# Second product of the second block's MLP by 2x2 blocks: seven block products per group in place of eight

## The chip, the cores and the metric

The kernel runs on one core of a Trainium2 chip. The core has TensorE (PE) for matrix products, which reads SBUF and writes PSUM; VectorE (DVE), ScalarE (ACT) and GpSimd (POOL) for elementwise work; and SyncE (SP), which here issues the loads of the weights. Each engine takes its instructions in order, and waits at the head of its own queue for semaphores of the others. The metric is the device time of one execution in microseconds (us); less is better. A measurement of this kernel can tell about 0.5% (some 6 us) from no change.

## The reference, cut to what matters

Two transformer blocks run one after the other on 512 tokens of width 1024, in float32. The change lies in the MLP of the second block, whose hidden width is 4096:

```
def _sq_relu_mlp(h, w1, w2):
    return jnp.square(jax.nn.relu(h @ w1)) @ w2
```

Its result is normalised by its rms, multiplied by a gain and added to the tokens; that is the kernel's output.

## The kernel before

**Products.** Every float32 operand is held as two parts, hi + lo, that TensorE takes in one pass each (`split`, L146: ACT copies the high part, L147, and DVE subtracts it for the low part, L148). A product is then three matmuls, hi·hi, hi·lo and lo·hi (`mm3`, L150 to L154).

**The MLP** (`mlp`, called by `dense_two`, name m2). The hidden width is 32 chunks of 128. `up(j)` makes chunk j of the first product, 128 hidden columns for all 512 tokens: 24 matmuls of 512 columns (for the first five chunks 48 of 256). ACT takes the relu (L843), DVE multiplies (L844), and the result is split into hi and lo in a tile `hid` of four chunks; three such tiles rotate. After eight chunks the second product of the group follows: two halves of 512 output columns, four tiles of 128 tokens, eight chunks, three matmuls each, so 192 matmuls for a group and 768 in all. The sum of a group stays in PSUM; ACT copies the first group's to `y` (L1278) and DVE adds the later ones to it (L1280). `y` is one tile [128, 1024] for each 128 tokens.

**Weights.** Each weight tile [128, 1024] comes by a DMA of 512 KB from SP's queue into one of two buffers (`raw`), and is split by ACT and DVE into hi and lo tiles, five of each (`wh`, `wl`). In the first four chunks of each MLP GpSimd does the subtraction in DVE's place (`WPJ`). In this MLP a tile of the first product serves 24 matmuls and one of the second product 24.

**The order.** A scheduler orders each engine's queue when the kernel is built; the program is written chunk by chunk and group by group. GpSimd has nothing from the fourth chunk of this MLP until the sums of squares at its end.

**The end.** With the last group, done token tile by token tile, `evac2` takes the sum of squares of `y` (ACT, L1243), multiplies by the gain (DVE, L1288), gets 1 / rms (GpSimd, L1245 to L1248), adds to the tokens (DVE, L1255) and stores.

Of the kernel before, what the change touches and what calls it, by code (L numbers as in the profile page):

```python
# [129 lines left out]
class Build:  # L130
    def __init__(self, tc, a, out):
        self.tc, self.nc, self.a, self.out = tc, tc.nc, a, out
        self.last_turn = None

# [1 line left out]
    def ps(self, tag, name):  # L136
        """the next of the tag's banks"""
# [7 lines left out]
    def split(self, hi, lo, src, eng=None):  # L145
        """src = hi + lo exactly, both parts fit the one-pass format"""  # L146
# [3 lines left out]
    def mm3(self, out, lh, ll, rh, rl, start, stop):  # L150
        mm = self.nc.tensor.matmul
# [10 lines left out]
    def weights(self, name, srcs, a, b, gain=None, eng=None):  # L162
        """hi/lo parts [128, a, b] of weights (times a gain [128, a] of the rows); srcs: (column offset, DRAM view [128, a, width])"""
# [82 lines left out]
    def columns(self, name, rows):  # L246
        """rows of the modulation, 128 columns to a partition"""
# [980 lines left out]
    def dense_two(self):  # L1228
# [46 lines left out]
        def evac2(grp, half, t, acc):  # L1275
            cols = slice(half * 512, half * 512 + 512)
            if grp == 0:
                ac(out=y[t][:, cols], in_=acc, func=AF.Copy)  # L1278
                return
# [40 lines left out]
```

## Time and profile before

| | us |
|---|---|
| median of three runs | 1274.99 |
| the three runs | 1271.56, 1274.99, 1276.72 |
| span of the profiled execution | 1270.8 |
| start of the second product's first matmul, group 0 | 951.81 |
| end of the last matmul | 1263.1 |
| busy in the whole span: PE / DVE / ACT / POOL | 1227.1 / 750.8 / 539.2 / 257.5 |

No time is given for the profiled execution itself other than its span; the span lies 4.2 us under the median of the runs, since it leaves out what lies before the first and behind the last instruction, and since executions differ. The MLP in question takes the span from about 910 us to its end. Busy times are read engine by engine in a stretch of time; "x" is the number of instructions. A matmul is recorded with its latency (0.39 us), and the next one begins 0.23 us later, so their cost is read from the distance of their starts.

### The profile page before, as it was taken

The page shows a single profiled execution, that of the slowest core. Times are in us where ns is not written, and L with a number is a line of the kernel's source. Part 1 is how long each engine was busy: PE and PEld are TensorE (multiplying, and loading weights), DVE is VectorE, ACT ScalarE, POOL GpSimd, SP SyncE. Part 2 cuts the span into 40 slices and gives each one's busy share as a digit, 9 for nine tenths or more (in the row PEclk, how much of TensorE's full clock was granted, in tenths as well). Part 3 has the DMA queues.
Part 4 walks back from the last instruction along what each step waited for, and adds up shares of the span by engine and source line. Part 5 has one row for each costly group of instructions (what it writes and reads, how often), then busy time and mean ns, then how long its engine had stood idle before and what let it go on. Part 6 is the DMA issues. An engine that isn't in the chain of part 4 may idle for free. (4 is left out here: it accounts for less than half of the span.)

```text
span 1270.8 us, 16908 instructions
## 1 busy us (share of the span) xinstructions
PE 1227.1 (97%) x6388; PEld 1027.8 (81%) x6388; DVE 750.8 (59%) x1320; ACT 539.2 (42%) x1032; POOL 257.5 (20%) x328
## 2 busy tenths in 40 slices
PE   7889999999999999999999999999999999999997
PEld 7889887779888788888888777778888888888886
DVE  4799666597897854336364567564752343433534
ACT  6677555434223324235263556454652331422431
POOL 3877551261020000000023114212400000000001
PEclk9899999999999999999999999999999999999999
DMA  5232121464678733143254122215232322412412
GB/s 163 64 73 68 26 63 67 133 186 148 198 239 257 234 100 116 63 131 122 67 176 129 51 67 74 64 59 178 82 117 83 100 100 67 130 69 67 149 50 84
DMA packets 147290, 140.22 MB, mean 110 GB/s; under 512 B 14025, under 2 KB 115160, under 8 KB 147208
## 3 DMA queue, kind: packets, MB, share of 16 engines
q1 hardware_dynamic: 143384, 131.02, 33.4%
q0 software_dynamic: 3824, 8.12, 2.1%
q8 instruction: 50, 0.82, 0.3%
q14 instruction: 32, 0.26, 0.1%
HBM read 134.85 MB, written 4.26 MB: 109 GB/s over the span
## 5 line engine op out<-in xcount | busy, mean ns | idle before, releaser
L898 DVE SCALAR_TENSOR_TENSOR macc<-mod,silu_c,macc 128x1024 f32<-128x1024 f32 x56 | 76.7, 1379 | 13.8 <-DMA mod<-in_w_mod_dram 13.7
L1245 POOL TENSOR_SCALAR ss<-ss 128x1 f32<-128x1 f32 x4 | 1.8, 442 | 328.5 <-ACT sk L1243 328.5
L1280 DVE TENSOR_TENSOR y<-m2d,y 128x512 f32<-128x512 f32 x24 | 16.6, 691 | 60.4 <-PE m2d L154 60.3
L975 DVE SCALAR_TENSOR_TENSOR xa<-m1d,r,xa 128x512 f32<-128x512 f32 x32 | 23.8, 745 | 37.2 <-PE m1d L154 37.2
L147 ACT ACTIVATE m2hid<-m2sq 128x512 fp32r<-128x512 f32 x32 | 20.2, 631 | 38.9 <-DVE m2sq L844 38.9
L147 ACT ACTIVATE m1hid<-m1sq 128x512 fp32r<-128x512 f32 x32 | 20.0, 629 | 38.1 <-DVE m1sq L844 38.1
L918 POOL DMA_DIRECT2D modrows<-mrow x8 | 3.9, 492 | 147.3 <-DVE mrow L916 92.8
L148 DVE TENSOR_TENSOR m2hid<-m2sq,m2hid 128x512 fp32r<-128x512 f32 x32 | 22.1, 691 | 19.0 <-ACT m2hid L147 18.9
L148 DVE TENSOR_TENSOR npl<-t,nph 128x512 fp32r<-128x512 f32 x32 | 21.7, 681 | 16.4 <-ACT nph L147 16.3
L181 POOL TENSOR_SCALAR w<-w,g_attn 128x384 f32<-128x384 f32 x20 | 26.1, 1314 | 11.2 <-DMA w<-in_w_in_dram 6.6
L148 DVE TENSOR_TENSOR m1hid<-m1sq,m1hid 128x512 fp32r<-128x512 f32 x32 | 21.9, 686 | 9.1 <-ACT m1hid L147 9.1
L194 POOL TENSOR_SCALAR p<-p,d 128x512 f32<-128x512 f32 x8 | 14.0, 1752 | 56.6 <-DVE d L1116 26.3
L683 DVE TENSOR_REDUCE mb<-sb 128x1 f32<-128x128 f32 (+3 forms) x32 | 15.6, 486 | 16.7 <-PE sb L680 16.6
L1115 ACT ACTIVATE p<-s,m 128x512 f32<-128x512 f32 x32 | 22.0, 688 | 6.2 <-DVE m L1113 6.2
L685 ACT ACTIVATE pb<-sb,mb 128x128 f32<-128x128 f32 (+3 forms) x32 | 16.8, 525 | 16.4 <-DVE mb L683 16.1
L843 ACT ACTIVATE m1re<-m1up 128x512 f32<-128x512 f32 x32 | 18.6, 582 | 9.0 <-PE m1up L154 8.7
L1069 POOL TENSOR_TENSOR tb<-G,nam 128x256 f32<-128x256 f32 x24 | 17.7, 765 | 22.6 <-DVE m L1109 12.5
L147 ACT ACTIVATE nph<-t 128x512 fp32r<-128x512 f32 x32 | 19.0, 595 | 7.4 <-PE t L1126 7.2
L844 DVE SCALAR_TENSOR_TENSOR m1sq<-m1up,m1re 128x512 f32<-128x512 f32 x32 | 21.8, 681 | 0.1
L844 DVE SCALAR_TENSOR_TENSOR m2sq<-m2up,m2re 128x512 f32<-128x512 f32 x32 | 21.8, 682 | 0.0
L1126 PE MATMUL t<-ident,p 128*128 128x128 f32 x128 | 18.4, 276 | 1.9 <-DVE npl L148 1.9
L147 ACT ACTIVATE pbh<-tb 128x128 fp32r<-128x128 f32 (+3 forms) x32 | 13.8, 434 | 14.9 <-PE tb L703 14.7
(1856 smaller groups left out, 4521.8 us busy)
## 6 DMA issues: line engine op xcount, KB each, us to landing
mod<-in_w_mod_dram SPq DMA_DIRECT2D x48, 512.0 KB, 4.5
m1u<-in_w_up_dram SPq DMA_DIRECT2D x32, 512.0 KB, 4.5
m1d<-in_w_down_dram SPq DMA_DIRECT2D x32, 512.0 KB, 3.6
m2u<-in_w_mlp_in_dram SPq DMA_DIRECT2D x32, 512.0 KB, 4.2
m2d<-in_w_mlp_out_dram SPq DMA_DIRECT2D x32, 512.0 KB, 3.4
w<-in_w_in_dram SPq DMA_DIRECT2D x16, 512.0 KB, 4.2
w<-in_w_in_dram SPq DMA_DIRECT2D x48, 128.0 KB, 2.6
o1w<-in_w_out_dram SPq DMA_DIRECT2D x8, 512.0 KB, 3.6
```

Source lines behind the costliest of these rows:

```text
L147: self.nc.scalar.activation(out=hi, in_=src, func=AF.Copy)
L148: (eng or self.nc.vector).tensor_tensor(out=lo, in0=src, in1=hi.bitcast(F32), op=ALU.subtract)
L181: eng.tensor_scalar(out=rv[:, i], in0=rv[:, i], scalar1=g, scalar2=None, op0=ALU.mult)
L685: ac(out=pr[:, 0:n], in_=s[:, 0:n], func=AF.Exp, bias=m[:, 0:1], accum_out=den[:, 0:1])
L843: ac(out=r, in_=acc, func=AF.Relu)
L844: nc.vector.scalar_tensor_tensor(out=s, in0=acc, scalar=0.0, in1=r, op0=ALU.max, op1=ALU.mult)
L898: nc.vector.scalar_tensor_tensor(out=accs[s], in0=rw, scalar=sc[:, s, k:k + 1], in1=accs[s], op0=ALU.mult, op1=ALU.add)
L975: nc.vector.scalar_tensor_tensor(out=x[t][:, cols], in0=acc, scalar=r2[:, t:t + 1], in1=x[t][:, cols], op0=ALU.mult, op1=ALU.add)
L1069: nc.gpsimd.tensor_tensor(out=tb[:, h, y], in0=G[:, h, ::-1, o:o + 32][:, :, ::-1], in1=nam[:, y, :].unsqueeze(1).to_broadcast([P, 8, 32]) ...
L1115: ac(out=pr, in_=s, func=AF.Exp, bias=m[:, 2:3], accum_out=den[:, 0:1])
L1126: nc.tensor.transpose(out=tps[:, j * P:(j + 1) * P], in_=pr[:, j * P:(j + 1) * P], identity=self.ident)
L1280: nc.vector.tensor_tensor(out=y[t][:, cols], in0=acc, in1=y[t][:, cols], op=ALU.add)
```

## The change

The second product takes groups of four chunks (512 of the hidden width) in place of eight. In a group the hidden activations A are four blocks, A11 and A12 for the first 256 tokens, A21 and A22 for the others, and the weights B four blocks of 256 rows by 512 columns. Winograd's form of Strassen's scheme gives the four blocks of A·B by seven block products of sums of blocks. A block product is 2 token tiles x 2 chunks x 3 = 12 matmuls of 512 columns, so a group has 84, where four chunks had 96 before; 672 in all in place of 768.

The sums are made on GpSimd. For each pair of chunks four sums of A blocks (128x256 each, `operands`); for each group four differences of B blocks (128x1024, written over b11 and b12); and the two products that enter several blocks of the result are added to `y` by GpSimd, in eight additions of 128x512 a group. ACT and DVE now split seven weight tiles for four chunks in place of four, and 1792 columns for each pair of chunks in place of 1024. DVE adds the other products to `y`, straight from PSUM. `y` is zeroed by GpSimd while the first half of `dense_two` runs. Banks 0 to 4 of PSUM serve the seven products in place of 0 to 2, the buffers of the output projection's weights become one ring of four (tag ex) that later holds b11, b12, b22 and b21, and tiles st (the squares) and S (the sums) share a ring of three (tag xr). The work at the end of a token tile is split by halves of the columns (`done`).

```diff
+        def operands(p, st):
+            sums = ep.tile([P, 4, 256], F32, tag="xr", name=f"{name}S{p}", bufs=3)
+            a11, a21, a12, a22 = st[:, 0, 0:256], st[:, 0, 256:512], st[:, 1, 0:256], st[:, 1, 256:512]
+            pt(out=sums[:, 0], in0=a21, in1=a22, op=ALU.add)
+            pt(out=sums[:, 2], in0=a11, in1=a21, op=ALU.subtract)
+            pt(out=sums[:, 1], in0=sums[:, 0], in1=a11, op=ALU.subtract)
+            pt(out=sums[:, 3], in0=a12, in1=sums[:, 1], op=ALU.subtract)
...
+            self.split(hi[:, 0], lo[:, 0], a11)
+            self.split(hi[:, 1:3].rearrange("p o t -> p (o t)"), lo[:, 1:3].rearrange("p o t -> p (o t)"), st[:, 1])
+            self.split(hi[:, 3:7], lo[:, 3:7], sums)
...
+        def down(g):
+            last = g == NG - 1
+            b11, b12, b22, b21 = [block(g, r, c) for r, c in ((0, 0), (0, 1), (1, 1), (1, 0))]
...
+            for tau, acc in times(1, 0, b11):
+                p1[tau] = ep.tile([P, 512], F32, tag="v", name=f"{name}c{g}{tau}", bufs=2)
+                ac(out=p1[tau], in_=acc, func=AF.Copy)
+                for c in (hi_, lo_):
+                    pt(out=y[tau][:, c], in0=y[tau][:, c], in1=p1[tau], op=ALU.add)
+            pt(out=b11, in0=b12, in1=b11, op=ALU.subtract)
+            for tau, acc in times(5, 3, b11):
+                tt(out=y[tau + 2][:, hi_], in0=acc, in1=y[tau + 2][:, hi_], op=ALU.add)
+            pt(out=b11, in0=b22, in1=b11, op=ALU.subtract)
+            for tau, acc in times(6, 4, b11):
+                tt(out=y[tau][:, hi_], in0=acc, in1=y[tau][:, hi_], op=ALU.add)
+            for tau, acc in times(3, 6, b22, ps[5]):
+                tt(out=y[tau][:, hi_], in0=acc, in1=y[tau][:, hi_], op=ALU.add)
...
+            pt(out=b12, in0=b22, in1=b12, op=ALU.subtract)
+            for tau, acc in times(7, 5, b12, ps[6]):
+                u3[tau] = spare[:, tau]
+                tt(out=u3[tau], in0=acc, in1=p1[tau], op=ALU.add)
+                for c, e in ((hi_, tt if last else pt), (lo_, pt)):
+                    e(out=y[tau + 2][:, c], in0=y[tau + 2][:, c], in1=u3[tau], op=ALU.add)
...
+            pt(out=b11, in0=b21, in1=b11, op=ALU.subtract)
+            for tau, acc in times(4, 2, b11):
+                tt(out=y[tau + 2][:, lo_], in0=acc, in1=y[tau + 2][:, lo_], op=ALU.add)
...
+            for tau, acc in times(2, 1, b21):
+                tt(out=y[tau][:, lo_], in0=acc, in1=y[tau][:, lo_], op=ALU.add)
...
+        for p in range(3):
+            if 2 * p >= NSP:
+                self.rings["s"] = s_banks
+            up(p)
+        self.rings["s"] = s_banks
+        for g in range(NG):
+            down(g)
+            for p in (2 * g + 3, 2 * g + 4):
+                if p < 2 * NG:
+                    up(p)
```

`times(q, o, b, banks)` splits b into a weight tile w and runs product q with operand number o of both pairs of the group; with `banks` it goes on in the banks of an earlier product, after DVE has read them.

The order moves on DVE, in the middle of the MLP. Names: u17 is the weight tile of chunk 17, d200 that of the second product (group 2, half 0, rows 0), sq the squares, hid the split activations. Before, one place of DVE's queue:

```order
L148 TENSOR_TENSOR m2u23l<-m2u_10363,m2u23h 128x1024
L844 SCALAR_TENSOR_TENSOR m2sq_10209<-m2up_10183,m2re_10208 128x512
L148 TENSOR_TENSOR m2hid_10109<-m2sq_10209,m2hid_10109 128x512
L148 TENSOR_TENSOR m2d200l<-m2d_10400,m2d200h 128x1024
L844 SCALAR_TENSOR_TENSOR m2sq_10246<-m2up_10220,m2re_10245 128x512
L148 TENSOR_TENSOR m2hid_10109<-m2sq_10246,m2hid_10109 128x512
L148 TENSOR_TENSOR m2d201l<-m2d_10434,m2d201h 128x1024
L844 SCALAR_TENSOR_TENSOR m2sq_10284<-m2up_10257,m2re_10283 128x512
```

The same place of DVE's queue now; w35 is the weight tile of group 3, product 5, and S the sums of A blocks:

```order
L149 TENSOR_TENSOR m2w31l<-m2d_10187,m2w31h 128x1024
L910 SCALAR_TENSOR_TENSOR m2sq_10029<-m2up_10036,m2sq_10029 128x512
L149 TENSOR_TENSOR m2hid_10101<-m2sq_10029,m2hid_10101 128x256
L149 TENSOR_TENSOR m2w35l<-m2d_10187,m2w35h 128x1024
L910 SCALAR_TENSOR_TENSOR m2sq_10029<-m2up_10069,m2sq_10029 128x512
L149 TENSOR_TENSOR m2hid_10101<-m2sq_10029,m2hid_10101 128x512
L149 TENSOR_TENSOR m2w36l<-m2d_10187,m2w36h 128x1024
L149 TENSOR_TENSOR m2hid_10101<-m2S_10096,m2hid_10101 128x1024
L149 TENSOR_TENSOR m2w33l<-m2d_10191,m2w33h 128x1024
L910 SCALAR_TENSOR_TENSOR m2sq_10108<-m2up_10115,m2sq_10108 128x512
```

What moved: the splits of weights stand closer together, a split of sums that GpSimd must have made has come between, and the weight tiles of products 5 and 6 are now differences that GpSimd makes from the tile that DVE has just split.

On GpSimd, before, these are neighbours: the last subtraction of the fourth chunk's weights and the sums of squares of the last token tiles, then those of the MLP's end:

```order
L148 TENSOR_TENSOR m2u3l<-m2u_9058,m2u3h 128x1024
L1247 TENSOR_SCALAR ssy_8443<-ssy_8443 128x1
L1248 TENSOR_TENSOR ssy_8443<-ssy_8443,nhalf 128x1
L1245 TENSOR_SCALAR ssx_8742<-ssx_8742 128x1
L1247 TENSOR_SCALAR ssx_8742<-ssx_8742 128x1
```

Now GpSimd has this between them, for each group; here the rows of group 3 from its first difference of B blocks (L945, L955, L948, L963 are differences of B, L883 to L886 sums of A, L944 and L960 additions to y):

```order
L945 TENSOR_TENSOR m2d_10187<-m2d_10189,m2d_10187 128x1024
L884 TENSOR_TENSOR m2S_10096<-m2sq_10029 128x256
L955 TENSOR_TENSOR m2d_10189<-m2d_10191,m2d_10189 128x1024
L948 TENSOR_TENSOR m2d_10187<-m2d_10191,m2d_10187 128x1024
L883 TENSOR_TENSOR m2S_10096<-m2sq_10029 128x256
L885 TENSOR_TENSOR m2S_10096<-m2S_10096,m2sq_10029 128x256
L886 TENSOR_TENSOR m2S_10096<-m2sq_10029,m2S_10096 128x256
L963 TENSOR_TENSOR m2d_10187<-m2d_10193,m2d_10187 128x1024
L884 TENSOR_TENSOR m2S_10175<-m2sq_10108 128x256
L944 TENSOR_TENSOR y_8429<-y_8429,m2c_10206 128x512 x2
L883 TENSOR_TENSOR m2S_10175<-m2sq_10108 128x256
L944 TENSOR_TENSOR y_8430<-y_8430,m2c_10217 128x512 x2
```

After these come L885, L886 and the four L960 of the group. What moved: GpSimd's queue, empty here before, holds twenty instructions a group, each with two inputs in SBUF. In the last group the order is another one; GpSimd's queue there:

```order
L948 TENSOR_TENSOR m2d_11372<-m2d_11376,m2d_11372 128x1024
L884 TENSOR_TENSOR m2S_11360<-m2sq_11293 128x256
L963 TENSOR_TENSOR m2d_11372<-m2d_11378,m2d_11372 128x1024
L944 TENSOR_TENSOR y_8429<-y_8429,m2c_11391 128x512 x2
L944 TENSOR_TENSOR y_8430<-y_8430,m2c_11402 128x512 x2
L883 TENSOR_TENSOR m2S_11360<-m2sq_11293 128x256
L885 TENSOR_TENSOR m2S_11360<-m2S_11360,m2sq_11293 128x256
L886 TENSOR_TENSOR m2S_11360<-m2sq_11293,m2S_11360 128x256
```

What moved: there the additions of product 1 to `y` stand ahead of the sums of the last pair.

## Rows read from the trace of the kernel before

**Rows 1.** The page: its head line.

```profile
span 1270.8 us, 16908 instructions
```

**Rows 2.** Busy time by stretch: stretch, length, PE busy (x instructions), granted clock, DMA; a sum.

```profile
951.81:1263.12 311.31, 311.29 (x1345) 1.00 0.29 90
...
sum 240.00, PE 240.00 PEld 194.83 DVE 90.11 ACT 73.51 POOL 0.00; mean PE 40.00 PEld 32.47 DVE 15.02 ACT 12.25 POOL 0.00
```

**Rows 3.** Groups by line and shape, DVE, 930 to 1271: count, busy, mean ns.

```profile
L148 DVE TENSOR_TENSOR m2hid<-m2sq,m2hid 128x512 fp32r<-128x512 f32 x32 | 22.1, 691 | 19.0 <-ACT m2hid L147 18.9
L844 DVE SCALAR_TENSOR_TENSOR m2sq<-m2up,m2re 128x512 f32<-128x512 f32 x30 | 20.5, 682 | 0.0
L1280 DVE TENSOR_TENSOR y<-m2d,y 128x512 f32<-128x512 f32 x24 | 16.6, 691 | 60.4 <-PE m2d L154 60.3
L148 DVE TENSOR_TENSOR m2d001l<-m2d,m2d001h 128x1024 fp32r<-128x1024 f32 x1 | 1.2, 1226 | 1.0 <-ACT m2d001h L147 1.0
```

**Rows 4.** Groups by line, ACT, the same stretch.

```profile
L147 ACT ACTIVATE m2hid<-m2sq 128x512 fp32r<-128x512 f32 x31 | 19.6, 631 | 38.9 <-DVE m2sq L844 38.9
L843 ACT ACTIVATE m2re<-m2up 128x512 f32<-128x512 f32 x30 | 17.4, 579 | 0.0
L147 ACT ACTIVATE m2u10h<-m2u 128x1024 fp32r<-128x1024 f32 x1 | 1.1, 1063 | 0.3 <-PE m2d L154 0.3
```

**Rows 5.** Tiles that GpSimd writes: count, least/median/most ns, first and last start, shapes.

```profile
L1069 POOL TENSOR_TENSOR tb<-G,nam x24: 707/724/1707, 679.4 to 771.5; 128x256 f32<-128x256 f32 x24
L940 POOL TENSOR_TENSOR xg<-xa,g_mlp x4: 1270/1280/2272, 238.7 to 257.9; 128x512 f32<-128x512 f32 x4
L148 POOL TENSOR_TENSOR m1u1l<-m1u,m1u1h x1: 2400/2400/2400, 274.2 to 274.2; 128x1024 fp32r<-128x1024 f32 x1
L546 POOL MEMSET lfx<- x1: 525/525/525, 17.7 to 17.7; 128x512 f32 x1
```

**Rows 6.** GpSimd in order of time, three places: start, duration, instruction.

```profile
255.17 2.77 POOL L148 TENSOR_TENSOR m1u0l<-m1u,m1u0h 128x1024 fp32r<-128x1024 f32 x1 [3.03 <-ACT m1u0h L147]
...
274.19 2.40 POOL L148 TENSOR_TENSOR m1u1l<-m1u,m1u1h 128x1024 fp32r<-128x1024 f32 x1
276.56 3.33 POOL L148 TENSOR_TENSOR m1u2l<-m1u,m1u2h 128x1024 fp32r<-128x1024 f32 x1
...
885.66 2.40 POOL L148 TENSOR_TENSOR m2u0l<-m2u,m2u0h 128x1024 fp32r<-128x1024 f32 x1
888.02 2.83 POOL L148 TENSOR_TENSOR m2u1l<-m2u,m2u1h 128x1024 fp32r<-128x1024 f32 x1
```

**Rows 7.** DVE in order of time, at the same places and alone.

```profile
254.41 1.27 DVE L898 SCALAR_TENSOR_TENSOR macc<-mod,silu_c,macc 128x1024 f32<-128x1024 f32 x1
255.60 0.68 DVE L148 TENSOR_TENSOR hT<-n_1t,hT 128x512 fp32r<-128x512 f32 x1
256.21 0.67 DVE L938 TENSOR_TENSOR xa<-o,xa 128x512 f32<-128x512 f32 x1
...
274.66 6.32 DVE L898 SCALAR_TENSOR_TENSOR macc<-mod,silu_c,macc 128x1024 f32<-128x1024 f32 x2
...
880.75 1.41 DVE L1255 SCALAR_TENSOR_TENSOR xb<-y,ssy,xb 128x512 f32<-128x512 f32 x2 [0.41 <-POOL ssy L1248]
...
885.73 5.68 DVE L1255 SCALAR_TENSOR_TENSOR xb<-y,ssy,xb 128x512 f32<-128x512 f32 x2 [0.20 <-POOL ssy L1248]
```

**Rows 8.** The chain that ended last, from 1262: start, length, what.

```profile
1262.87 0.25 PE m2d L154
...
1266.43 0.66 DVEq L1305
```

**Rows 9.** Waits of PE, 840 to 912: total, times, longest.

```profile
PE m2up L153 <- DVE h2T L148: 1.5, 1, 1.5
PE n_1t L216 <- DVE n_1x L232: 1.0, 1, 1.0
```

**Rows 10.** Busy time by stretch: PE, PEld, DVE, ACT, POOL, granted clock, DMA.

```profile
905.00:910.00 5.00, 5.00 (x36) 5.00 (x35) 4.13 (x6) 2.54 (x8) 3.38 (x6) 0.78 0.35 95
```

**Rows 11.** The page: loads from SP's queue, KB each, us from issue to landing.

```profile
m2u<-in_w_mlp_in_dram SPq DMA_DIRECT2D x32, 512.0 KB, 4.2
```

More of the change, by code (lines that the diff above doesn't have):

```diff
@@ L133, in __init__ @@
         self.last_turn = None
+        self.xrb = 2
     def ps(self, tag, name):
@@ L148, in split, with mm3, mm @@
         (eng or self.nc.vector).tensor_tensor(out=lo, in0=src, in1=hi.bitcast(F32), op=ALU.subtract)
-    def mm3(self, out, lh, ll, rh, rl, start, stop):
-        mm = self.nc.tensor.matmul
+    def mm3(self, out, lh, ll, rh, rl, start, stop, again=False):
+        def mm(**kw):
+            self.nc.tensor.matmul(**kw, skip_group_check=again)
         mm(out=out, lhsT=lh, rhs=rh, start=start, stop=False)
@@ L227, in mod_T @@
         nc = self.nc
-        xr = self.ep.tile([P, D], F32, tag="xr", name=name + "x", bufs=2)
+        xr = self.ep.tile([P, D], F32, tag="xr", name=name + "x", bufs=self.xrb)
         if r is None:
@@ L771, in out_proj_rows @@
                 else:
-                    own = [self.ep.tile([P, 1024], F32R, tag=f"w{x}{i}", name=f"{n}{x}", bufs=1) for x in "hl"]
-                rv = self.ep.tile([P, 1024], F32, tag="wraw", name=n + "r", bufs=2) if len(tiles) in XR else None
+                    own = [self.ep.tile([P, 1024], F32R, tag="ex", name=f"{n}{x}", bufs=4) for x in "hl"]
+                rv = self.ep.tile([P, 1024], F32, tag="ex", name=n + "r", bufs=4) if len(tiles) in XR else None
                 tiles.append(self.parts(n, self.fetch(n, srcs, 2, 512, rv), 2, 512, own=own))
@@ L1269, in evac1, with done @@
                 self.mod_T(x[t], g, hT, t, f"n4_{t}", rx)
+                nc.gpsimd.memset(y[t], 0.0)
         self.out_proj_rows(a["w_out_2"][0], self.mixT, evac1, "o2", KPS2)
[L1271 to L1275 removed]
+        self.banks(a=(0, 1, 2, 3, 4), s=S2)
+        ss2 = [self.small("ss2", f"ss2{t}") for t in range(NT)]
+        def done(t, half):
             cols = slice(half * 512, half * 512 + 512)
[L1277 to L1292 removed]
+            r = squares(y[t][:, cols], ss2[t], 1 - half, f"sk{half}{t}")
+            nc.vector.tensor_tensor(out=y[t][:, cols], in0=y[t][:, cols], in1=gg[:, 1, cols], op=ALU.mult)
+            if half == 0:
+                for _, c in post(t, [y[t][:, 0:512], y[t][:, 512:1024]], r):
+                    nc.sync.dma_start(out=self.out[0, t * P:(t + 1) * P, c], in_=x[t][:, c])
+        self.mlp_seven(hT, a["w_mlp_in_2"][0], a["w_mlp_out_2"][0], y, done, gg[:, 0, :].rearrange("p (a b) -> p a b", a=2), "m2")
 _INS = ['x', 'attn_norm_g', 'w_in', 'b_forget', 'q_norm_a', 'k_norm_a', 'sink_logits', 'q_norm_b', 'k_norm_b', 'w_out',
```

73 lines of the change are left out of this document (58 added, 15 removed).

## The prediction

> **What bounds the kernel now.** First the busy times by stretch. From the second product's first matmul to the last one TensorE is busy 311.29 of 311.31 us at the full clock (1.00, the 2.4 GHz level), with 1345 records of 1344 matmuls [rows 2]: 0.2316 us each. In 240 us of this DVE is busy 90, ACT 74 and GpSimd 0 [rows 2]. So TensorE alone bounds this stage; a matmul less is 0.2316 us less, as long as the others keep up. Then the groups by line of the three other engines, for what their work costs [rows 3 to 5], and last GpSimd and DVE side by side in time, at the few places where both work [rows 6, 7]. The reader is to see there that they don't work side by side.
>
> **What is removed.** 768 - 672 = 96 matmuls of 512 columns: 96 x 0.2316 = 22.2 us off the path. Four chunks took TensorE 192 matmuls, 44.5 us; they take 180 now (96 of the first product, 84 of the second), 41.7 us. Everything else in the change is work for engines that had room, so the question is whether it fits into 41.7 us a group.
>
> **What is added, for four chunks.**
> - ACT: 11 weight tiles at 1.06 us, 4 relus at 0.58, the hidden splits (by columns, from 0.63 for 512 and 1.06 for 1024, some 2.1 a pair) and two copies of some 0.6 [rows 4]: 11.7 + 2.3 + 4.2 + 1.2 = 19.4 us. It fits.
> - DVE, with two inputs in SBUF: 11 weight tiles at 1.226, and for each of two pairs splits of 256, 512 and 1024 columns (an estimated 0.42 by the two rows, 0.69, 1.23): 13.5 + 4.7 = 18.2 us. With one input in PSUM: 4 squares at 0.682 and 12 additions at 0.691: 11.0 us [rows 3]. Together 29.2 us. By itself it fits.
> - GpSimd: 4 differences of 128x1024 at 2.40, 8 additions of 128x512 at 1.28, 8 sums of 128x256 at 0.72 [rows 5]: 9.6 + 10.2 + 5.8 = 25.6 us. By itself it fits.
>
> **The two together.** At 274.19 GpSimd has two subtractions of 128x1024; DVE at 274.66 two instructions with two SBUF inputs, 1.27 each when alone. They take 6.32 us in place of 2.54, and GpSimd's second 3.33 in place of 2.40 [rows 6, 7]. At 885.66 the same with 128x512 on DVE: 5.68 in place of 1.41 [rows 6, 7]. So one waits until the other's instruction is through, and they take turns. From 274.19 to 280.98 (274.66 + 6.32) are 6.79 us for two of each: less 4.80 for GpSimd, 1.0 us for each of DVE's; at the other place 5.75 - 4.80, 0.48 each. An instruction of DVE with an operand in PSUM doesn't wait: at 255.60 and 256.21 they take 0.68 and 0.67 while GpSimd works [rows 6, 7]. The Trainium skill has this as a rule that speaks against the change ("SBUF — State Buffer", section "Who interferes with whom": an instruction of VectorE with two SBUF inputs and one of GpSimd that reads SBUF exclude each other for the whole instruction); the trace agrees. The same page's section "A bandwidth-pool intuition that's wrong (but worth ruling out)" has the waiting one finish some 115 ns late (measured there on something else); by that estimate 17 turns a group would add 2 us a group, 12 us in all, while the rows show 0.27 us won at each turn. I go by the rows.
>
> In each group the port is then held for 25.6 us by GpSimd and 13 x 1.0 + 2 x 0.48 + 2 x 0.2 (estimated for 256 columns) = 14.4 by DVE: 40.0 us, of TensorE's 41.7. That is the lower bound, TensorE's 41.7. The upper, if DVE and GpSimd never worked at the same time: 29.2 + 25.6 = 54.8. Between them the order decides, so I follow one group through the two queues as they now stand, with GpSimd's durations as above, DVE's of 1.14 and 0.60 (neighbours start 0.07 to 0.09 us before the other's end [rows 7]) where nothing holds it and 1.0 and 0.48 behind a wait, and 0.09 us from engine to engine. Clock 0 is the end of the group's first weight split (w31 in the order shown). GpSimd makes b12-b11 until 2.5; the next hidden split on DVE waits for it, 2.7; a sum of A, 3.3, b22-b12, 5.7; DVE's split of product 5's weights, ready to run at 3.7, waits until 5.7 and ends at 6.7. Only then may GpSimd make b22-b11, to 9.1; hidden split 9.6; a sum 10.2; one more 11.0, split of product 6, 12.0; last sum 12.7; b21-b11, 15.0, and only then the split of the sums, 16.0. Then products 3 and 7, squares and hidden parts to 21.1, GpSimd's additions of product 1 to 23.0, product 4's split 24.0, sum, hidden part 25.1, more additions between product 2's split (27.4) and DVE's additions to 29.3, the next weights 30.4, the second pair's sums (ACT first) 33.4, 35.2, product 7 to 36.4, then GpSimd's last four additions in turns with two weight splits and DVE's additions to the same y tiles, which wait for them, to 44.2; the next group's first split ends at 45.3. The load for the fourth weight tile (4.2 us [rows 11], its buffer free at 35.2) makes it some 0.5 later. So **a group takes about 46 us**, against 41.7 of TensorE: 4.3 us a group in which TensorE waits for operands or free banks. That is even above the 44.5 of before.
>
> Six groups have this shape (groups 0 to 5, each with four chunks of the first product). When they begin, DVE and GpSimd are ahead by some 5 us, which the first group uses up: 6 x 4.3 - 5 = **+20.8**. Bounds: 6 x 0 = 0, and 6 x 13.1 = 79; I take the chain's own value, and for the range 41.7 to 48.5 a group (0 to +36), since at 54.8 even the PSUM instructions, which rows 7 show to run through, would have to wait.
>
> **The last group, the end, the start.** In group 7 GpSimd's additions of product 1 (4 x 1.28) stand ahead of the sums that product 5 needs. From the end of the last first-product matmul: product 1's second tile 2.8, copy 3.5, additions to 8.3, of which the first two run earlier, so 7.2; three sums 9.3, ACT 10.4, DVE 11.6. TensorE has 30 matmuls that need none of it, 6.9 us. **+5**, from 3 to 10 with turns at the port.
> At the end, four token tiles finish within product 4's and product 2's last 5.5 us, in place of one each 5.5 us. From the end of product 4's first tile, 4.2 us ahead of the last matmul, DVE has 19 instructions of some 0.68 [rows 3, 7]: 12.9, so 8.7 us behind the last matmul. Before it was done at 1267.09, 4.0 behind it [rows 8]. **+5**, from 3 to 7.
> Zeroing y, four of 128x1024 on GpSimd, an estimated 1 us each (twice 0.525 [rows 5]), stands ahead of the 1 / rms of each token tile, in a place where TensorE waits 1.0 and 1.5 us for the tokens [rows 9]: **+1**, from 0 to 3. The clock was at half (0.78 mean [rows 10]) for some 3 us after those waits; waits of that size can now come in each group, but TensorE waits there for DVE anyway, so I set 0.
> The PSUM banks (five for seven products) and the loads (the same bytes) I cost at 0: banks come free with DVE's additions, which the chain holds.
>
> Sum: -22.2 + 20.8 + 5 + 5 + 1 = +9.6. Against the profile's span: 1270.8 + 9.6 = 1280.4; the median of the runs lies 4.2 above the span [rows 1], so 1285.
>
> **The rivals.**
> - *The lookahead hides the turns, faster.* Five weight tiles of each part and three of hidden ones let DVE run ahead, and 40.0 is below 41.7. Then stalls are 0: -22.2 + 0 + 4 + 4 + 0 = -14, 1261. For it: the bare port time fits, and TensorE has never waited in this stage. Against it: each of products 5, 6 and 4 needs a split, a difference, a split in a row, and the port idles in between. Chance 0.25, with what falls just short of it in the next.
> - *It comes out even.* A group at 43 to 44.5: stalls 3 to 12 us, 1270 to 1279. Chance 0.22.
> - *The forecast*, 45 to 47 a group: 1281 to 1291. Chance 0.31.
> - *Slower still.* DVE's splits lose two turns each when GpSimd's next instruction is already queued, so that DVE's order is driven by GpSimd. It decides once a group passes 47.5 us: stalls over 30, 1295 to 1310. For it: the rows show only two neighbours of each, never a long queue of both. Chance 0.20.
> - *Without effect on the matmuls*: the sums could have cost the first product's order on TensorE. The order shows 672 and no more transposes; 0.02, at 1275.
>
> The range leaves out the faster tail below 1260 and the slower above 1306. Faster by over 0.5% (under 1268.6; less can't be told from no change): 0.26. Within: 0.24. Slower (over 1281.4): 0.50.
>
> **What would show it.** In the profile after: 672 second-product matmuls, at 0.23 us from start to start; low-part splits (L149) of 128x1024 on DVE at a mean well above 1.23 us, 1.7 or more, while the additions from PSUM stay near 0.69; GpSimd busy some 200 us more; TensorE waiting for DVE at products 5, 4 and 7, some 4 us for each 46. It would be wrong if TensorE is busy throughout and the splits take 1.23 (the rival that is faster), or if groups take 48 and more.

## The result, and the profile after

The changed kernel takes 1301.6 us (median of 4 runs, 1300.4 to 1303.6) against 1273.3 (4 runs): a ratio of 1.0226, 95% interval 1.0200 to 1.0252. It is slower, as forecast, but by nearly three times as much: its profiled execution spans 1299.2 us, 28.4 more than the one before [rows 1], where the sum said +9.6.

The page of the changed kernel, its head, the busy times and the chain that ended last, by engine:

```profile
span 1299.2 us, 17090 instructions
PE 1218.5 (94%) x6292; PEld 1006.7 (77%) x6292; DVE 904.1 (70%) x1434; ACT 575.2 (44%) x1080; POOL 523.2 (40%) x490
POOL 14%; DVE 7%; PE 5%; issue 4%; ACT 3%; DVEq 0%; POOLq 0%; ACTq 0%
```

GpSimd leads the chain. Where the time went is best read from the first matmul of each group's product 1 (weight tile w01 in group 0, w11 in group 1, and so on). The tiles' view gives count, least/median/most ns, and the first and last start:

```profile
L154 PE MATMUL m2p<-m2w01h,m2hid x8: 392/395/467, 939.8 to 948.9; 128*128 128x512 f32 x8
L154 PE MATMUL m2p<-m2w11h,m2hid x8: 389/392/397, 991.4 to 993.9; 128*128 128x512 f32 x8
L154 PE MATMUL m2p<-m2w21h,m2hid x8: 390/392/404, 1033.2 to 1035.7; 128*128 128x512 f32 x8
L154 PE MATMUL m2p<-m2w31h,m2hid x8: 390/397/401, 1078.7 to 1081.2; 128*128 128x512 f32 x8
...
L154 PE MATMUL m2p<-m2w61h,m2hid x8: 390/397/401, 1215.2 to 1217.8; 128*128 128x512 f32 x8
L154 PE MATMUL m2p<-m2w71h,m2hid x8: 390/564/793, 1249.6 to 1255.5; 128*128 128x512 f32 x8
```

A group with four chunks of the first product should take 180 x 0.2316 = 41.7 us, group 6 with two chunks 30.6, group 7 with none 19.5. The last matmul ends at 1284.8. The kernel before makes chunks 6 and 7 of the first product, 48 matmuls, ahead of its second product's first matmul, where the changed kernel makes them later; so the same point lies at 951.81 - 48 x 0.2316 = 940.7 there. Its end lies 7.7 behind its last matmul [rows 1, 2].

| | measured | over its matmuls | predicted |
|---|---|---|---|
| matmuls removed | | -22.2 | -22.2 |
| up to the first product 1 | 939.8 (940.7) | -0.9 | +1 |
| group 0 | 51.6 | +9.9 | groups 0 to 5: +20.8 |
| group 1 | 41.8 | 0 | |
| groups 2 to 5, each | 45.5 | 4 x 3.8 = +15.3 | |
| group 6 | 34.4 | +3.8 | 0 |
| group 7 | 35.2 | +15.7 | +5 |
| last matmul to the end | 14.4 (7.7) | +6.7 | +5 |
| sum | | +28.3 | +9.6 |

DVE (first fence) and GpSimd (second) in order of time in group 3, which repeats every 45.5 us; start, duration, instruction, idle time before it and its releaser. L945, L955, L948 and L963 are the differences for products 5, 7, 6 and 4, L883 to L886 the sums of hidden tiles, L149 the low parts.

```profile
1065.02 1.22 DVE L149 TENSOR_TENSOR m2w31l<-m2d,m2w31h 128x1024 fp32r<-128x1024 f32 x1
1066.15 0.68 DVE L910 SCALAR_TENSOR_TENSOR m2sq<-m2up,m2sq 128x512 f32<-128x512 f32 x1
1067.32 1.68 DVE L149 TENSOR_TENSOR m2hid<-m2sq,m2hid 128x256 fp32r<-128x256 f32 x1 [0.49 <-ACT m2hid L148]
1069.84 3.21 DVE L149 TENSOR_TENSOR m2w35l<-m2d,m2w35h 128x1024 fp32r<-128x1024 f32 x1 [0.84 <-ACT m2w35h L148]
...
1076.66 1.23 DVE L149 TENSOR_TENSOR m2w36l<-m2d,m2w36h 128x1024 fp32r<-128x1024 f32 x1 [0.58 <-ACT m2w36h L148]
1080.43 2.32 DVE L149 TENSOR_TENSOR m2hid<-m2S,m2hid 128x1024 fp32r<-128x1024 f32 x1 [2.54 <-ACT m2hid L148]
...
1110.54 1.22 DVE L149 TENSOR_TENSOR m2w41l<-m2d,m2w41h 128x1024 fp32r<-128x1024 f32 x1
```

```profile
1066.31 2.40 POOL L945 TENSOR_TENSOR m2d<-m2d,m2d 128x1024 f32<-128x1024 f32 x1 [2.54 <-DVE m2w31l L149]
1068.67 0.92 POOL L884 TENSOR_TENSOR m2S<-m2sq 128x256 f32<-128x256 f32 x1
1069.57 2.40 POOL L955 TENSOR_TENSOR m2d<-m2d,m2d 128x1024 f32<-128x1024 f32 x1
1073.13 2.40 POOL L948 TENSOR_TENSOR m2d<-m2d,m2d 128x1024 f32<-128x1024 f32 x1 [1.16 <-DVE m2w35l L149]
...
1079.26 2.41 POOL L963 TENSOR_TENSOR m2d<-m2d,m2d 128x1024 f32<-128x1024 f32 x1
```

These rows show DVE and GpSimd taking turns. The split m2w35l starts 0.27 us after L955, sits until L955 ends at 1071.97, and ends 1.08 later at 1073.05: 3.21 us for an instruction of 1.22. GpSimd's next difference (L948) waits for exactly this split, since it overwrites the tile. The additions with an operand in PSUM stay at 0.68.

### The profile page after: what moved, and what is told of

The parts are those of the page before. It is cut to its first block, busy times and chain, and to the rows that moved or that the text cites. A ratio compares the mean times of both kernels' runs of the same rounds, so it can differ in the third digit from the quotient of the medians.

```text
span 1299.2 us, 17090 instructions
## 1 busy us (share of the span) xinstructions
PE 1218.5 (94%) x6292; PEld 1006.7 (77%) x6292; DVE 904.1 (70%) x1434; ACT 575.2 (44%) x1080; POOL 523.2 (40%) x490
## 5 line engine op out<-in xcount | busy, mean ns | idle before, releaser
L960 POOL TENSOR_TENSOR y<-y,g_post 128x512 f32<-128x512 f32 x30 | 51.2, 1735 | 34.9 <-DVE g_post L958 34.9
L944 POOL TENSOR_TENSOR y<-y,m2c 128x512 f32<-128x512 f32 x32 | 55.0, 1738 | 7.8 <-ACT m2c L942 7.8
L149 DVE TENSOR_TENSOR m2hid<-m2sq,m2hid 128x256 fp32r<-128x256 f32 (+1 forms) x32 | 44.9, 1407 | 10.4 <-ACT m2hid L148 10.4
L148 ACT ACTIVATE m2hid<-m2S 128x1024 fp32r<-128x1024 f32 x16 | 16.9, 1059 | 72.8 <-POOL m2S L886 72.8
L149 DVE TENSOR_TENSOR m2hid<-m2S,m2hid 128x1024 fp32r<-128x1024 f32 x16 | 26.7, 1671 | 31.1 <-ACT m2hid L148 31.1
L148 ACT ACTIVATE m2hid<-m2sq 128x256 fp32r<-128x256 f32 (+1 forms) x32 | 16.7, 524 | 62.2 <-DVE m2sq L910 62.0
L154 PE MATMUL pj<-w_0h,xnT 128*128 128x384 f32 (+1 forms) x96 | 31.4, 364 | 4.0 <-ACT pjs L411 2.9
L149 DVE TENSOR_TENSOR npl<-t,nph 128x512 fp32r<-128x512 f32 x32 | 21.7, 681 | 16.5 <-ACT nph L148 16.3
L154 PE MATMUL pj<-w_2h,xnT 128*128 128x384 f32 (+1 forms) x96 | 29.4, 344 | 1.0 <-ACT w_2h L186 1.0
L154 PE MATMUL pj<-w_1h,xnT 128*128 128x384 f32 (+1 forms) x96 | 29.9, 351 | 0.0
L154 PE MATMUL pj<-w_3h,xnT 128*128 128x384 f32 (+1 forms) x96 | 29.1, 346 | 0.3 <-ACT w_3h L148 0.3
L149 DVE TENSOR_TENSOR m1hid<-m1sq,m1hid 128x512 fp32r<-128x512 f32 x32 | 22.0, 687 | 9.1 <-ACT m1hid L148 9.1
```

The source lines that it names most:

```text
L148: self.nc.scalar.activation(out=hi, in_=src, func=AF.Copy)
L149: (eng or self.nc.vector).tensor_tensor(out=lo, in0=src, in1=hi.bitcast(F32), op=ALU.subtract)
L154: self.nc.tensor.matmul(**kw, skip_group_check=again)
L944: pt(out=y[tau][:, c], in0=y[tau][:, c], in1=p1[tau], op=ALU.add)
L960: e(out=y[tau + 2][:, c], in0=y[tau + 2][:, c], in1=u3[tau], op=ALU.add)
```

## The experiments

All executions from here on have nearly the same instructions up to the second product, but reach its first product 1 at 934.6 to 944.4. So beside the span I give the **stage**, from that matmul to the end: 330.1 us before, 359.4 after. A group is the mean of groups 2 to 5: 45.5 after, 41.7 without waits. Each experiment is one execution, if no number of runs is given.

**Only writes on GpSimd.** The edit leaves out each of GpSimd's sums, differences and additions but for four columns, and writes constants in their place (the new body in words):

```
-pt = nc.gpsimd.tensor_tensor
+def pt(out, in0, in1, op):
+    (the operation on the first four columns)
+    (memsets of about the same length)
+    (the operation on the first four columns again)
```

> Every sum, difference and addition of the changed kernel's second product on GpSimd is left out but for four of its columns; in its place GpSimd writes constants for about the same time (0.525 us for 512 columns), between two 4-column instructions that keep what it waits for and who waits for it. So GpSimd is as busy and stands at the same places of the chains, but hardly reads SBUF. Theory (turns: an instruction of DVE with two SBUF inputs and one of GpSimd that reads SBUF wait for each other's end): DVE's 1024-wide splits of L149 go back from a mean of 1.67 to 1.2 us, a steady group from 45.5 to 41.7 to 42.5 us, and the span from 1299 to 1270 to 1280. Rival (GpSimd's own durations in the chain split, difference, split set the group): splits 1.2, but a group stays at 45 to 46 and the span at 1295 to 1300. If writes too exclude DVE: nothing changes, neither the splits nor the groups.

Stage 320.8, span 1260.5, group 42.4. The groups by line, 1040 to 1220, of DVE in this kernel and then in the changed one (x count, busy, mean ns, idle before):

```profile
L149 DVE TENSOR_TENSOR m2hid<-m2S,m2hid 128x1024 fp32r<-128x1024 f32 x9 | 11.0, 1223 | 17.1 <-ACT m2hid L148 17.1
```

```profile
L149 DVE TENSOR_TENSOR m2hid<-m2S,m2hid 128x1024 fp32r<-128x1024 f32 x8 | 14.2, 1776 | 14.7 <-ACT m2hid L148 14.7
```

Here the splits take 1.22 us again, beside a GpSimd that is busy 105.7 of the 180 us. Most of that is writing, by its groups of the same stretch:

```profile
L885 POOL MEMSET m2scr<- 128x512 f32 x101 | 53.1, 526 | 3.3
L883 POOL MEMSET m2S<- 128x252 f32 x65 | 17.0, 307 | 0.1
```

So it is GpSimd's reading that holds DVE up: 1.223 us beside writes, 1.776 beside reads. The Trainium skill has this as a rule ("SBUF — State Buffer", "Who interferes with whom"): two SBUF inputs on VectorE collide with an instruction of GpSimd that reads SBUF, not with one that only writes it. The trace agrees. GpSimd's durations in the chain, the rival, stood nearly unchanged, and a group kept 0.7 of its 3.8 us. The span is lower than the 1270 to 1280 I had expected, because the first group (43.3) and the last (20.8) lost their turns as well.

**The port's load alone, on the kernel before.** Behind each hidden chunk of the second block, after a subtraction of four columns that waits for the chunk:

```
...
+for n in (1024, 512, 512, 256, 256):
+    nc.gpsimd.tensor_tensor(out=scr[:, 0:n], in0=scr[:, 0:n], in1=scr[:, 0:n], op=ALU.subtract)
```

> The kernel before, whose instruction order on the other engines stays as it is, and on GpSimd, behind each of the second block's 32 hidden chunks, five additional subtractions on a tile that nobody reads any more: one of 1024, two of 512, two of 256 columns, 6.4 us a chunk, 25.6 for four chunks, as much as in the changed kernel. The load on the port is there, the dependence of TensorE's operands on GpSimd is not. Theory (it is the fixed order of turns through the chain that costs, the port itself has room): DVE's splits lengthen to 1.6 us or more, TensorE still waits for nothing, span 1269 to 1274. Rival (the shared port alone is the bound, whatever the order): a group of four chunks takes 3 to 4 us longer, span 1295 to 1303.

The span is 1267.9, the stage 330.2 against 330.1. By stretch, 940 to 1180 (PE, PEld, DVE, ACT, POOL busy, clock), and DVE's group of hidden splits, 930 to 1270:

```profile
940.00:1180.00 240.00, 240.00 (x1037) 194.89 (x1037) 113.29 (x98) 69.69 (x88) 150.78 (x136) 1.00 0.30 90
```

```profile
L148 DVE TENSOR_TENSOR m2hid<-m2sq,m2hid 128x512 fp32r<-128x512 f32 x31 | 35.0, 1131 | 19.2 <-ACT m2hid L147 19.2
```

GpSimd is in its instructions for 63% of the time (its waits for a turn included), DVE's hidden split goes from 0.69 [rows 3] to 1.13 us, its weight splits to a mean of 1.68, and TensorE is busy for all of the 240 us. The same amount of work on the port costs nothing when no operand passes through GpSimd and DVE has slack. This run takes away both at once, the passage of operands through GpSimd and DVE's other work (113 of 240 us busy here, 144 of 180 in the changed kernel), so by itself it doesn't say which of the two makes the turns costly.

**Which part of the order.** Seven kernels each change one thing, or a few, in what GpSimd and DVE do. The sums of hidden tiles on DVE (four lines like this one):

```
-pt(out=sums[:, 0], in0=a21, in1=a22, op=ALU.add)
+tt(out=sums[:, 0], in0=a21, in1=a22, op=ALU.add)
```

> The changed kernel, but the four sums of the hidden tiles (128x256, eight for a group) are DVE's in place of GpSimd's: GpSimd 25.6 to 19.8 us a group, DVE 29.2 to 32.6. Theory (turns in the chain): the chain loses the turns at the sums, a steady group takes 42.5 to 44 in place of 45.5, the first group (12 sums, 51.6 us) 45 to 48, the last 30 to 33; span 1275 to 1285. Rival (DVE's own time decides): groups 45.5 and above, span 1299 to 1306. Rival (GpSimd's time decides): 41.7 to 42, span 1270 to 1276.

Product 1's additions on DVE, from PSUM:

```
-pt(out=y[tau][:, c], in0=y[tau][:, c], in1=p1[tau], op=ALU.add)
+tt(out=y[tau][:, c], in0=acc, in1=y[tau][:, c], op=ALU.add)
```

> The changed kernel, but product 1 is added to y in all groups by DVE from PSUM (4 x 0.69 us a group) in place of GpSimd (4 x 1.28): GpSimd 25.6 to 20.5 us a group, DVE 29.2 to 32.0. Theory of turns in the chain: these additions only stand in turns with two weight splits at the group's end, so a steady group gains 1 to 2 us (43.5 to 44.5), the last one 6 as with its additions alone moved: span 1278 to 1286. Rival (DVE is as much the bound: with the sums on DVE it was busy 92% of the time and nothing was won in a group): 45 to 46, span 1291 to 1295.

A fifth tile for the blocks, `bx`, so that no difference overwrites what DVE has yet to split for the product before (and the first three differences are written ahead of product 1's additions):

```
-pt(out=b11, in0=b12, in1=b11, op=ALU.subtract)
+pt(out=bx, in0=b12, in1=b11, op=ALU.subtract)
...
-pt(out=b11, in0=b22, in1=b11, op=ALU.subtract)
+pt(out=b11, in0=b22, in1=bx, op=ALU.subtract)
```

> The changed kernel with the same operations on the same engines, but a fifth tile of 128x1024 for the blocks of the second matrix (room from the squares' scratch, now one tile of half the width): the differences for products 5, 6, 7 no longer overwrite what DVE has yet to split for the product before, so GpSimd can make three of them in a row, ahead of DVE. Everything reads the port as long as before. Theory (it is the chain split, difference, split, difference that costs, not the port's load): a steady group falls from 45.5 to 42.5 to 43.5 us, span 1284 to 1289. Rival (total time at the port: 40.0 us of 41.7 by the prediction, so any order stalls): 45 to 46, span 1297 to 1301.

The square on ACT:

```
-nc.vector.scalar_tensor_tensor(out=st[:, f], in0=acc, scalar=0.0, in1=st[:, f], op0=ALU.max, op1=ALU.mult)
+ac(out=st[:, f], in_=st[:, f], func=AF.Square)
```

> The changed kernel, but the square of the relu is made by ACT (Square of its own result), so DVE has 2.7 us a group less; all of GpSimd's work stays. Theory (turns through GpSimd set the group, not how full DVE is): 44.5 to 45.5 a steady group, span 1292 to 1299. Rival (DVE's fullness): 42.5 to 43.5, span 1278 to 1286.

Sums and differences on DVE and the square on ACT (`tt` for `pt` in these lines, and the edit above):

> The changed kernel with all sums and differences on DVE and the square on ACT; on GpSimd stay only the additions to y (8 x 1.28 = 10.2 us a group), which no operand of TensorE waits for. DVE has 29.2 + 3.4 + 4.9 - 2.7 = 34.8 us a group. Theory (GpSimd costs where TensorE's operands go through it in turns with DVE): a steady group 41.7 to 42.3, span 1268 to 1277. Rival (any reading by GpSimd beside a full DVE costs): 43 to 44.5, span 1278 to 1288.

Sums and product 1's additions on DVE, the square on ACT:

> The changed kernel with the sums of the hidden tiles and the additions of product 1 on DVE (the latter from PSUM), and the square of the relu on ACT (Square of its own result, some 0.6 us) in place of DVE: GpSimd 14.7 us a group (differences and the additions of u3), DVE 29.2 + 3.4 + 2.8 - 2.7 = 32.7, ACT 19.4 + 2.4 = 21.8. Theory (turns in the chain; fewer turns, DVE no fuller than with the sums alone): a steady group 42 to 44, span 1270 to 1282. Rival (DVE with its waits is the bound): 44.5 to 46, span 1288 to 1295.

And nothing left on GpSimd, the square on ACT:

```
-pt = nc.gpsimd.tensor_tensor
+pt = nc.vector.tensor_tensor
```

> The changed kernel with nothing on GpSimd in the second product's groups: sums, differences and additions on DVE, the square on ACT. DVE alone has 29.2 + 8 x 0.42 + 4 x 1.23 + 8 x 0.69 - 2.7 = 40.3 us of work a group, and no turns. Theory (turns): all splits of L149 take 1.23 us, and a group is 42 to 44 us, limited by DVE's 40.3 and TensorE's 41.7; span 1272 to 1284. Rival (an engine that is full to 97% stalls in whatever order): 45 us and more, span 1292 to 1305.

| kernel | GpSimd, DVE a group, us of work | group | stage | span |
|---|---|---|---|---|
| changed | 25.6, 29.2 | 45.5 | 359.4 | 1299.2 |
| sums on DVE | 19.8, 32.6 | 45.2 | 356.9 | 1294.4 |
| square on ACT | 25.6, 26.5 | 44.4 | 352.8 | 1287.4 |
| fifth tile | 25.6, 29.2 | 44.2 | 344.8 | 1288.1 |
| product 1's additions on DVE | 20.5, 32.0 | 43.1 | 341.8 | 1282.6 |
| only additions on GpSimd, square on ACT | 10.2, 34.8 | 42.6 | 328.1 | 1271.0 |
| only differences and u3's additions on GpSimd, square on ACT | 14.7, 32.7 | 42.0 | 333.7 | 1274.5 |
| nothing on GpSimd, square on ACT | 0, 40.3 | 41.8 | 323.1 | 1267.5 |

The fifth tile changes only the order, with every load the same, and a group gains 1.3 us; I had expected 2 to 3. The two kernels with nearly the same loads (19.8 and 32.6; 20.5 and 32.0) differ by 2.1 us a group. That fits the turns: the sums become instructions with two SBUF inputs on DVE, which still take turns, and the additions from PSUM don't; no run separates this from their places in the queues. With the sums on DVE my expectation failed: a group gained 0.3, not 1.5 to 3. With product 1's additions on DVE it gained more than the 1 to 2 that I had expected, 2.4. Of the kernel with the sums on DVE, the stretch 1040 to 1220, and the waits of PE from 930 to 1260 (total, times, longest; 8.3 of the 12.9 us lie in that stretch):

```profile
1040.00:1220.00 180.00, 171.68 (x718) 136.17 (x717) 166.02 (x164) 71.50 (x91) 88.19 (x48) 0.98 0.30 93
```

```profile
PE m2p L154 <- DVE y L947: 12.9, 7, 2.7
```

DVE is held 92% of the time, and TensorE waits for the additions (L947) that free the PSUM banks, because DVE's queue is late. So the rival "DVE's fullness" has its part: taking 2.7 us off DVE (square on ACT) gave 1.1, which lies between what the two theories expected of it. And a DVE that is nearly full but never takes turns does no harm: in the last row DVE has 40.3 us of work in 41.8, by the sum of durations (neighbours overlap, so it is busy 158.5 of 180 us). The group and the span came out a little under the 42 and 1272 that I had expected at the least, and TensorE is busy throughout (the same stretch):

```profile
1040.00:1220.00 180.00, 180.00 (x777) 145.75 (x776) 158.52 (x213) 87.96 (x112) 0.00 (x0) 1.00 0.32 98
```

Two rows speak against a reading by TensorE's operands alone. With only additions on GpSimd no operand passes through it, yet a group is 42.6 us, between the theory's 41.7 to 42.3 and the rival's 43 to 44.5. With only the differences and u3's additions on GpSimd the operands still go DVE, GpSimd, DVE, and splits still wait (m2w55l takes 2.51 us), yet TensorE is busy throughout, as the theory's 42 to 44 allowed:

```profile
1040.00:1220.00 180.00, 180.00 (x773) 144.61 (x772) 163.70 (x178) 87.93 (x112) 73.64 (x34) 1.00 0.32 100
```

The largest gain of a single edit, 2.4, is that of product 1's additions, which make no operand of TensorE. That the operands' passage is the dear part is therefore not shown. Each single edit shortened a group; what one turn costs depends on the order of both queues, and no run isolates it.

**The last group.** First only its additions of product 1 moved to DVE, as above but `if last`:

> The changed kernel, but in the last group the four additions of product 1 to y are DVE's, from PSUM (0.69 us each), no longer GpSimd's; the order of everything else stays but for some ten rows. Theory (in the last group these four additions, 7.4 us in turns, held up the sums that products 5, 3, 7, 4 and 2 need): the sums come at 1260 in place of 1266, TensorE's wait of 5.7 us before 1269.8 goes, the last group takes 28 to 30 us in place of 35.1, span 1292 to 1294. Rival (DVE is late there itself: its last square came only at 1260, behind a weight split, and it gets 2.8 us more to do): the wait only shrinks by 2, span 1297.

Then the whole group as eight block products, token tile by token tile, as before, and without the sums of its hidden tiles:

```
+if last:
+    for t in range(4):
+        for c, cs in ((1, hi_), (0, lo_)):
+            (12 matmuls of the four blocks into one bank)
+            tt(out=y[t][:, cs], in0=acc, in1=y[t][:, cs], op=ALU.add)
+            done(t, c)
+    return
```

> The changed kernel, but the last group's second product is made as in the kernel before: eight block products (96 matmuls in place of 84, +2.8 us), token tile by token tile, without sums, differences or GpSimd; groups 0 to 6 as changed. Theory (the last group's 35.2 us, and 14.4 from the last matmul to the end, come from its sums, its additions and from four token tiles that become ready together): from its first matmul to the last one 23 to 25 us, from there to the end 7.7 as before, group 6 a little shorter: span 1277 to 1282. Rival (the delay is handed on from groups 5 and 6, GpSimd being late): the last group stays at 29 to 31, span 1285 to 1290.

The first took 29.6 us in group 7 in place of 35.2 (span 1293.0), the second 22.4 and then 8.5 to the end in place of 14.4 (span 1277.2), both spans as the theory had them (the second's group a little below its 23 to 25). Group 6 didn't get shorter (35.1), which the theory had expected, but the last group, without sums, runs without a wait behind it, so nothing is handed on from group 6. GpSimd, DVE and PE at the decisive place of the changed kernel:

```profile
1259.03 7.38 POOL L944 TENSOR_TENSOR y<-y,m2c 128x512 f32<-128x512 f32 x4
1266.37 0.72 POOL L883 TENSOR_TENSOR m2S<-m2sq 128x256 f32<-128x256 f32 x1
...
1267.97 0.72 POOL L886 TENSOR_TENSOR m2S<-m2sq,m2S 128x256 f32<-128x256 f32 x1
```

```profile
1256.72 3.43 DVE L149 TENSOR_TENSOR m2w77l<-m2d,m2w77h 128x1024 fp32r<-128x1024 f32 x1
1260.07 0.68 DVE L910 SCALAR_TENSOR_TENSOR m2sq<-m2up,m2sq 128x512 f32<-128x512 f32 x1
1269.81 1.23 DVE L149 TENSOR_TENSOR m2hid<-m2S,m2hid 128x1024 fp32r<-128x1024 f32 x1 [5.76 <-ACT m2hid L148]
```

```profile
1264.11 0.80 PE L154 MATMUL m2p<-m2w74h,m2hid 128*128 128x512 f32 x1 [0.50 <-DVE m2hid L149]
1269.83 0.79 PE L154 MATMUL m2p<-m2w75h,m2hid 128*128 128x512 f32 x1 [4.93 <-ACT m2hid L148]
```

The four additions take 7.4 us in turns, the three sums behind them end at 1268.7, and TensorE stands until 1269.8. The rival of the first experiment, that DVE is late there itself, has its part too: in that run the sums end at 1262.3, but DVE is late with the additions it took over (its square comes at 1259.1 there, behind the turn of m2w77l), and TensorE waits 4.8 us for those (L945 is now their line). DVE in order of time, and PE's wait, in that run:

```profile
1255.85 3.37 DVE L149 TENSOR_TENSOR m2w77l<-m2d,m2w77h 128x1024 fp32r<-128x1024 f32 x1
1259.74 2.47 DVE L945 TENSOR_TENSOR y<-m2p,y 128x512 f32<-128x512 f32 x4
```

```profile
PE m2p L154 <- DVE y L945: 4.8, 1, 4.8
```

**The first group** as eight block products (the same edit under `g == 0`):

> The changed kernel, but the second product of the first group (group 0) is made by eight block products (96 matmuls, +2.8 us), without sums, differences or GpSimd; groups 1 to 7 as changed. In the changed kernel groups 0 and 1 took 51.6 + 41.8 us, 93.3, where the prediction had 5 us less than two groups of 45.5. Theory (group 0 is late because twelve sums and four differences fall on GpSimd at once there, and the waits let TensorE's clock fall): group 0 takes 44.5 to 46, group 1, for which GpSimd starts with nothing queued, 42 to 45.5, the others 45.5; span 1290 to 1296. Rival (whichever group is the first of its kind pays, since five weight tiles of lookahead have to be filled through the turns): group 0 44.5, group 1 49 to 52, span 1297 to 1303.

Group 0 took 44.6, group 1 41.8, the others 45.5 to 45.7: stage 352.7, span 1295.7, the theory's. Group 1 there runs without a wait, but not because the queues are faster in it. DVE's first splits for groups 1 and 2 in that run:

```profile
970.11 1.22 DVE L149 TENSOR_TENSOR m2w11l<-m2d,m2w11h 128x1024 fp32r<-128x1024 f32 x1
...
1015.94 1.22 DVE L149 TENSOR_TENSOR m2w21l<-m2d,m2w21h 128x1024 fp32r<-128x1024 f32 x1
```

DVE and GpSimd take 45.8 us for it, about as for the groups behind it; but w11 was ready 16.3 us before TensorE came to it (987.6), w21 only 12.2 (1029.4), so TensorE lived off a head start that was then used up. A head start of some 4 us is real. Group 0 of the changed kernel, where twelve sums and four differences fall together, doesn't have it: GpSimd there has no pause from 927.6 to 962.3.

**Both put together**: nothing on GpSimd, the square on ACT, the last group as eight block products.

> The changed kernel with nothing on GpSimd in the second product's groups and the square on ACT (a steady group took 41.8 us so, span 1267.5), and the last group's product in eight block products, token tile by token tile. Theory: the last group, 24.7 us there, costs 2.8 more for its 12 matmuls but has no wait, some 23 to 25; the end behind the last matmul goes from 15.0 to 7.7 as before; span 1256 to 1261, some 10 to 14 us faster than the kernel before. Rival (the end is set by DVE's queue, which is late by then): span 1263 to 1268.

It is 1259.0 us (median of 4, 1257.3 to 1262.0) against 1271.9 (7 runs), a ratio of 0.9905, interval 0.9876 to 0.9934: some 1% faster than the kernel before, and faster than the changed one. Its span of 1256.0 lies at the lower bound of the theory. The groups take 41.8 us, the last 22.4, the end 9.0, stage 314.8. Its chain that ended last, by engine:

```profile
PE 26%; DVE 1%; POOL 1%; ACT 1%; issue 0%; POOLq 0%; DVEq 0%; ACTq 0%
```

## Why the prediction came out as it did

- **The mechanism of a steady group was right.** Turns at a shared port, in the order of the two queues, set it: without GpSimd's reads 3.1 of the 3.8 us went, and the same reads beside a DVE with slack cost nothing.
- **The hand-followed group was right**, step by step. From the end of the split of w31 (1066.24) it had the first difference done at 2.5, product 5's split at 6.7, the next difference at 9.1, product 6's split at 12.0, the last difference at 15.0, the split of the sums at 16.0. The rows give 2.5, 6.8, 9.3, 11.7, 15.4, 16.5, and the next group's first split (w41) ends at 45.5, where it had 45.3. Its 45.3 to 45.8 for a group, taken as 46, measured 45.5: 3.8 a group over TensorE, not 4.3. A split that had waited ended 1.08 us behind GpSimd's end, in place of 1.22 alone. By the Trainium skill's 115 ns ("SBUF — State Buffer", section "A bandwidth-pool intuition that's wrong (but worth ruling out)"), taken for each turn, the estimate would have been 2 us a group more. The rows decide against that estimate.
- **The head start failed as a step.** I took 5 us off because the engines seemed ahead when the groups begin. They were behind: the first group lost 9.9 us, and only the second, which lost nothing, had a head start, of 3.8. For groups 0 to 5 that made +25.2 in place of +20.8 (0.5 x 6 less, 7.4 more).
- **Group 6 was left out.** The same chain runs in it; +3.8 where I had nothing.
- **The last group is the term that was mis-sized most**: +15.7 against 5 (3 to 10). The steps that failed are "additions to 8.3, of which the first two run earlier, so 7.2; three sums 9.3, ACT 10.4, DVE 11.6". From the end of the last first-product matmul (1249.57) product 1 ended at 6.4 in place of 2.8, since TensorE waited 1.1 and 0.9 us for hidden parts (their square stood on DVE behind a split that lost a turn, m2w75l, 2.44 us) and the clock fell. Its copies ended at 8.2 in place of 3.5. GpSimd's additions began at 9.5, behind the difference for product 4, which lost a turn as well (3.32 us), and took 7.4 in place of 5.1, to 16.8 in place of 7.2; the sums ended at 19.1, ACT at 20.2, DVE at 21.5. That is 9.9 us late, of the 10.7 that the term was short. The 30 matmuls of cover were spent on the way, between waits of 1.1, 0.9, 0.9, 1.7 and 0.5 us. GpSimd's difference in time:

```profile
1255.74 3.32 POOL L963 TENSOR_TENSOR m2d<-m2d,m2d 128x1024 f32<-128x1024 f32 x1 [1.56 <-DVE m2w76l L149]
```

- **The clock, set at 0, was not 0.** In the first and the last group the granted clock fell to its lower level (1.2 GHz). By stretch (PE, PEld, DVE, ACT, POOL busy, clock), in the first and the last group of the changed kernel:

```profile
950.00:960.00 10.00, 6.77 (x21) 5.15 (x22) 9.01 (x10) 5.22 (x7) 10.00 (x7) 0.83 0.17 53
...
1265.00:1270.00 5.00, 0.17 (x1) 0.17 (x2) 0.19 (x1) 1.06 (x1) 3.54 (x5) 0.50 0.00 0
1270.00:1275.00 5.00, 4.92 (x13) 3.57 (x14) 1.96 (x3) 0.64 (x1) 0.00 (x0) 0.61 0.00 0
```

From 1269.83 to 1274.82 twelve matmuls take 4.99 us in place of 2.78, from 1253.65 to 1256.81 seven 3.16 in place of 1.62, from 956.53 to 960.25 nine 3.72 in place of 2.08: 5.4 us in all, contained in the two groups' terms above. Before it fell TensorE had stood five times in the first group (1.3, 0.6, 1.2, 1.7 and 2.2 us), twice in the last (1.1 and 0.9) and there once more for 4.93. From 970 to 1250 the clock stayed at 1.00.
- **The end** was right in kind: +6.7 against 5 (3 to 7). **The start** cost nothing measurable (-0.9).
- **Of the signs named beforehand**, the splits (a mean of 1.68 us for 1024 columns, just under the 1.7 named), the additions (0.68 to 0.69), GpSimd's busy time (+266 us, of which some 205 is work by 8 x 25.6, and most of the rest turns) and 3.8 us of 45.5 lost by TensorE came out. The places of the waits did so only in part: in a steady group they stand at products 6, 4, 3 and 7, the longest (0.8 us) behind ACT's copy of product 1. The range (to 1306) held the time by luck, since it was made from steady groups of up to 48.5 us. The case "slower still" (1295 to 1310) gave the size, but not for its reason: no group passed 47.5 us but the first, and the longest weight splits of the steady and the last groups (3.2 and 3.43 us) waited for one instruction of GpSimd, not two.

What stays open is how the 3.8 us of a group divide: the single edits give 0.3, 1.1, 1.3 and 2.4, which add up to more than the whole, so they are not independent parts.

## What to carry to other kernels

Cost a steady loop by following the queues by hand, and do the same for the first and the last pass: 18 of the 19 us of this miss came from there (7.4 and 10.7; the other terms nearly cancel), with TensorE's clock down there as well. Before giving GpSimd work that reads SBUF, ask how much of DVE's work has two SBUF inputs, and whether either queue has slack to wait for the other. Two engines that take turns can be slower than one that is nearly full: with the square on ACT in both, 40.3 us on DVE alone gave 41.8 a group, 26.5 beside 25.6 on GpSimd 44.4. Less on GpSimd was harmless (14.7 beside 32.7: 42.0). And a trick that saves matmuls need not be used in every pass: leaving it out of the last group cost 2.8 us of matmuls and won 17.8 net (stage 359.4 to 341.6).

## What the hardware showed that I had not expected

- GpSimd's writes of constants didn't hold up DVE (1.223 us for a split that takes 1.226 alone), so the exclusion goes by what is read.
- GpSimd was in instructions that read SBUF for 63% of the time beside an unhurried DVE, without any loss to TensorE (240.00 of 240 us busy).
- In the first group TensorE waited 1.3, 0.6, 1.2, 1.7 and 2.2 us between 941.3 and 956.5, and its next eight matmuls started 0.43 us apart in place of 0.23, at half the clock. In the kernel with the sums on DVE, the stretch 950 to 960 shows a clock of 0.53, and its first group took 52.7 us, the longest of all.
